# Gate one-hots laid token by token in unit step, in a decoder trunk with product-key experts

## The chip, the cores and the metric

The kernel runs on one core of one Trainium2 chip. The metric is the device time of one execution in microseconds (us); lower is better. The five engines of the core have short names in the profile: PE is TensorE (PEld its weight loads), DVE is VectorE, ACT is ScalarE, POOL is GpSimd and SP is SyncE, which here only issues DMA transfers. Each engine works through its own list of instructions in order and waits on semaphores for the others.

## What is computed

A trunk of two layers over 512 tokens of width 1024. Layer 0 mixes tokens with a gated linear recurrence, layer 1 with latent attention; behind each comes a PEER layer, and this is the part that matters here. For every token and each of 8 heads, two small products with 128 keys each give two top-16 lists, and the best 16 of their sums give 16 experts out of 128 x 128 (index `e1 * 128 + e2`) with softmax gates. Each expert is one neuron, a row of `u_tab` and a row of `v_tab`:

```python
idx = e1 * N_KEYS + e2
g = jax.nn.softmax(cv, axis=-1).astype(h.dtype)
act = jax.nn.gelu(jnp.einsum('bcd,bchkd->bchk', hc, u_tab[ic]), approximate=False)
return jnp.einsum('bchk,bchkd->bcd', gc * act, v_tab[ic])
```

So each token uses 8 x 16 = 128 experts of 16384.

## The kernel before, in words

The kernel treats the four blocks of 128 tokens in two ways. For the last block it gathers the rows of the 128 chosen experts by indirect DMA (`gather_steps`, L1443), one expert of all 128 tokens per step, and VectorE does the dot product (L1457) or the weighted sum (L1462). For the other three blocks (384 tokens) it computes all 16384 experts densely on TensorE: in 128 steps `u_part` (L1111) multiplies 128 rows of the first table with the tokens and applies the GELU, and 128 steps of the last stage multiply the result by the gates (`weigh`, L1220) and by the second table (`v_part`, L1268). For that it needs the gates as a dense matrix, 128 x 128 per token, nearly all zero.

fp32 operands are split into a high and a low part of reduced fp32 (`split`, L162: L164 on ScalarE, L165 on VectorE), and three matmuls (L201 to L203) do one product. Each `u_part` loads 512 KB of the table (`raw`), splits it into `whi` and `wlo`, and runs 24 matmuls of 384 columns.

**The gate stage.** `gate_prep` (L990) runs once per block. It turns the indices e1, e2 and the gates g of 128 tokens, which lie with tokens on the partitions, by TensorE so that the 128 choices lie on the partitions and the tokens along the free dimension. ScalarE copies e1 and e2 out of PSUM as fp16 (L998, tile `et`) and the gates as fp32 (`gt`, L1001). VectorE writes the gates as two fp16 tiles that add up to them: rounded (L1004) and the rest (L1005), tile `gp`.

`gate_group` (L1008) builds the dense gates of 16 tokens in two halves of HT = 8 tokens. For each half VectorE does two operations of 2048 columns:

- L1022 writes `oo`: for each token and each of the 128 possible values, 1 where the index equals the value and else 0; 8 tokens x 128 values for e1, and the same for e2. The values come from the constant `iota_e`.
- L1024 writes `pr`: the e1 one-hots times the rounded gates, and times their rest.

Then TensorE does, per token, two matmuls of 128 x 128 in fp16 that add up in PSUM: the e2 one-hots as weights, the two halves of `pr` as the moving operand (L1032, and L193 in the helper `follow`). Four tokens fill a bank `wps`, ScalarE copies it into `stg` (L1035), and 16 tokens at a time go to scratch memory in DRAM (L1037). `oo` and `pr` have two buffers each, so a half can be written only when TensorE is done with the half before the last.

In memory the free dimension of `oo` and `pr` is ordered: group of 4 tokens, value, token within the four. The operand of one token (`oo[:, n4 + a, :, t]`, `pr[:, a, :, t]`) thus has a step of 4 elements, 8 bytes. VectorE reads the token operand of L1022 and L1024 as 4 neighbours, repeated over 128 values.

**Order of the work.** Per layer there are 24 calls of `gate_group`. Between them `peer` (L1196 to L1209) puts in two or three `u_part` each (50 over the stage), the decoding of the next block's choices, and 74 of the 256 gather steps of the last block. The order on each engine comes from the order of issue in the program, priorities and a timeline that the tile framework keeps; `issue_after` adds single constraints. `fill` (L253) runs matmuls on `iota_e` whose result is not used, between the layers.

Of the kernel before, what the change touches and what calls it, by code (L numbers as in the profile page):

```python
# [12 lines left out]
F16 = mybir.dt.float16  # L13
I32 = mybir.dt.int32
U32 = mybir.dt.uint32
AF = mybir.ActivationFunctionType
OP = mybir.AluOpType
# [4 lines left out]
P = 128  # L22
# [16 lines left out]
TG = 16  # L39
# [11 lines left out]
HT = 8  # L51
# [32 lines left out]
class Trunk:  # L84
# [25 lines left out]
    def setup(self):  # L110
        nc, c, io = self.nc, self.consts, self.io
        self.csil = c.tile([P, D], F32, name="csil")
        nc.scalar.dma_start(self.csil, bass.AP(tensor=io["c"].tensor, offset=io["c"].offset, ap=[[0, P], [1, D]]))
        self.x = self.state.tile([P, KC, T], F32, name="x")
        for k in range(0, KC, 2):
            nc.sync.dma_start(self.x[:, k:k + 2, :], io["xT"][:, k:k + 2, :])
        self.vecs = c.tile([P, NV], F32, name="vecs")
        nc.scalar.dma_start(self.vecs, io["vecs"])
        self.cst = c.tile([P, 4], F32, name="cst")
        nc.scalar.dma_start(self.cst, io["cst"])  # L120
        ii = c.tile([P, P], I32, name="ii")
        nc.gpsimd.iota(ii, pattern=[[1, P]], base=0, channel_multiplier=-1)
        self.ident = c.tile([P, P], F32, name="ident")
        nc.vector.tensor_scalar(self.ident, ii, 0.0, None, op0=OP.is_equal)
        self.ones = c.tile([P, 1], F32, name="ones")
        nc.vector.memset(self.ones, 1.0)
        self.iota_e = c.tile([P, P, 4], F16, name="iota_e")
        nc.gpsimd.iota(self.iota_e, pattern=[[1, P], [0, 4]], base=0, channel_multiplier=0,
                       allow_small_or_imprecise_dtypes=True)
        self.iota_m = c.tile([P, TOPK, TOPK], BF, name="iota_m")  # L130
        nc.gpsimd.iota(self.iota_m, pattern=[[1, TOPK], [0, TOPK]], base=0, channel_multiplier=0,
                       allow_small_or_imprecise_dtypes=True)
        self.eps = c.tile([P, 1], F32, name="eps")
        nc.vector.memset(self.eps, EPS)
        self.tiny = c.tile([P, 1], F32, name="tiny")
        nc.vector.memset(self.tiny, 1e-30)
        self.mod = c.tile([P, 112], F32, name="mod")
        self.xscr = self.dram.tile([P, KC, T], F32, name="xscr")
        self.gscr = self.dram.tile([DEPTH, SPILL, P, ND], F32, name="gscr")
        self.rscr = self.dram.tile([P, T], F32, name="rscr")  # L140
        self.mscr = self.dram.tile([P, NB, T], BF, name="mscr")
        self.wscr = self.dram.tile([DEPTH, NSG, P, P * TG], F32, name="wscr")
# [108 lines left out]
        return self.last_sq  # L251

    def fill(self, bank, n):  # L253
        e = self.iota_e.rearrange("p e t -> p (e t)")
        for _ in range(n):
            with self.tc.issue_after(self.tail):
                self.tail = self.nc.tensor.matmul(bank, e[:, :P], e, start=True, stop=True).ins
# [732 lines left out]
    def gate_prep(self, pool, e1, e2, g):  # L990
        nc = self.nc
        tp = self.bank("et")
        fl = "p h k -> p (h k)"
        for n, src in enumerate((e1, e2, g)):
            nc.tensor.transpose(tp[:, n * P:n * P + P], src.rearrange(fl), self.ident)
        by_group = [P, P // HT, 2, HT]
        et = pool.tile(by_group, F16, name="et", bufs=2)
        nc.scalar.activation(et.rearrange("p g a t -> p a g t"), tp[:, 0:2 * P].rearrange("p (a g t) -> p a g t", a=2, t=HT),  # L998
                             AF.Copy)
        gt = pool.tile([P, P], F32, name="gt", bufs=2)  # L1000
        nc.scalar.activation(gt, tp[:, 2 * P:3 * P], AF.Copy, scale=GSCALE)  # L1001
        gp = pool.tile(by_group, F16, name="gp", bufs=2)
        gt = gt.rearrange("p (g t) -> p g t", t=HT)
        nc.vector.tensor_copy(gp[:, :, 0, :], gt)  # L1004
        nc.vector.tensor_tensor(gp[:, :, 1, :], gt, gp[:, :, 0, :], op=OP.subtract)  # L1005
        return et, gp

    def gate_group(self, pool, l, b, sg, et, gp):  # L1008
        nc = self.nc
        n4 = HT // 4  # L1010
        shp = [P, 2 * n4, P, 4]
        io = self.iota_e.unsqueeze(1).to_broadcast(shp)
        stg = pool.tile([P, P, TG], F32, name="stg", bufs=2)
        for t0 in range(0, TG, HT):

            def toks(ap):
                g = ap[:, (sg * TG + t0) // HT].rearrange("p q t -> p (q t)")
                return g.rearrange("p (a t) -> p a t", t=4).unsqueeze(2).to_broadcast(shp)

            oo = pool.tile(shp, F16, name="oo", bufs=2)  # L1020
            pr = pool.tile(shp, F16, name="pr", bufs=2)
            nc.vector.tensor_tensor(oo, io, toks(et), op=OP.is_equal)  # L1022
            two = [P, 2, n4, P, 4]
            prod = nc.vector.tensor_tensor(pr.rearrange("p (q a) e t -> p q a e t", q=2),  # L1024
                                           oo[:, 0:n4].unsqueeze(1).to_broadcast(two),
                                           toks(gp).rearrange("p (q a) e t -> p q a e t", q=2), op=OP.mult)
            for a in range(n4):
                wps = self.bank("wps")
                for t in range(4):
                    w = oo[:, n4 + a, :, t]  # L1030
                    out = wps[:, t * P:t * P + P]
                    lead = nc.tensor.matmul(out, w, pr[:, a, :, t], start=True, stop=False).ins  # L1032
                    last = self.follow(lead, out, w, pr[:, n4 + a, :, t], stop=True)
                c = t0 + 4 * a
                nc.scalar.activation(stg[:, :, c:c + 4].rearrange("p e t -> p t e"),  # L1035
                                     wps.rearrange("p (t e) -> p t e", t=4), AF.Copy, scale=1.0 / GSCALE)
        nc.scalar.dma_start(self.wscr[l, b * (P // TG) + sg], stg.rearrange("p e t -> p (e t)"))  # L1037
        return last.ins, prod.ins
# [519 lines left out]
```

## Time and profile before

| | |
|---|---|
| Time, median of 3 runs | 3019.38 us (3011.92 to 3022.08) |
| The profiled execution | 3019.97 us, span 3018.1 us, mean granted clock 0.993 |
| Busy of the span | PE 98%, DVE 85%, ACT 46%, POOL 29% |
| Gate matmuls (L1032 and L193) | 2 x 768, from 468.0 to 2305.0 us |
| One-hots and products (L1022 and L1024) | 96 each, mean 1221 and 1219 ns |
| Copies out of PSUM (L1035) | 192, mean 1113 ns |
| DMA over the span | 813.71 MB, mean 270 GB/s |

A row of a group names line, engine, operation, output <- inputs, the shape as partitions x elements, the count; behind the bar stand busy time in us and the mean of one in ns, then the idle time of the engine just before them and what ended most of it. A row of one line or tile gives the shortest, median and longest duration in ns, then the first and the last start in us. A row of waits reads "engine, what waited, its line <- who released it: us in total, times, longest us". A row of windows gives start and end, then the length, the busy time of each engine with its count of instructions, the granted clock, the share of DMA and GB/s. A row of the chain in time order gives start, length and the line; a row of the timeline gives start, length from the first start to the last end, line, and how many instructions it merges.

### The profile page before, as it was taken

To read this page: it belongs to the slowest core of one execution; us is meant where nothing else is said; L and a number is where in the kernel's file an instruction comes from. 1 tells how busy PE (TensorE), PEld (TensorE's weight loads), DVE (VectorE), ACT (ScalarE), POOL (GpSimd) and SP (SyncE) were. 2 spreads that over 40 slices of the span, in tenths; PEclk is the share of its full clock that TensorE was granted. 3 is DMA by queue.
4 is the path that set the end of the run, shared out by engine and by line. 5 is a ranking of instruction groups with operands and counts; after the bars stand their busy time and mean duration, and the time that the engine had idled before them with its cause. 6 is when DMAs were issued, how large, how long until landed. Compare 5 with 4: busy or idle time off the path is not lost.

```text
span 3018.1 us, 43873 instructions
## 1 busy us (share of the span) xinstructions
PE 2958.0 (98%) x15680; PEld 2648.6 (88%) x15680; DVE 2565.2 (85%) x4887; ACT 1389.1 (46%) x2033; POOL 888.1 (29%) x718
## 2 busy tenths in 40 slices
PE   7999999999999999999999999999999999999998
PEld 5689999999888889998878799999999888899997
DVE  8989999898888878879878888989986777788888
ACT  4752255555433333333576742456554333333333
POOL 4000003344132234535334400023432111145542
PEclk9999999999999999999999999999999999999999
DMA  8544558899999999999324333379999999999996
GB/s 315 181 144 147 185 194 306 299 349 324 311 383 359 361 321 349 326 348 323 120 83 128 121 124 129 126 242 333 319 329 322 320 332 331 320 320 355 345 338 222
DMA packets 296218, 813.71 MB, mean 270 GB/s; under 512 B 33152, under 2 KB 130560, under 8 KB 289600
## 3 DMA queue, kind: packets, MB, share of 16 engines
q1 hardware_dynamic: 188928, 439.41, 42.8%
q0 software_dynamic: 78912, 287.34, 27.0%
q10 hardware_dynamic: 28160, 84.14, 7.1%
q8 instruction: 124, 2.03, 0.3%
q14 instruction: 94, 0.77, 0.1%
HBM read 727.44 MB, written 83.36 MB: 269 GB/s over the span
## 4 chain that ended last, share of the span: by engine, by line
PE 81%; DVE 11%; DMA 3%; issue 2%; ACT 2%; POOL 0%; ACTq 0%; SPq 0%; DVEq 0%; POOLq 0%
PE acc L203 12%; PE acc L202 12%; PE acc L201 11%; PE u L201 10%; PE u L202 10%; PE u L203 10%; PE wps L1032 3%; PE wps L193 3%; DVE wlo L165 2%; DVE ada_junk L153 1%; PE pq L202 1%; PE pq L203 1%; PE pq L201 1%; DMA ada_raw<-in_adaw_dram 1%; PE pv L834 1%
## 5 line engine op out<-in xcount | busy, mean ns | idle before, releaser
L1453 POOL DMA_INDIRECT grow<-in_u_dram,idx x256 | 361.2, 1411 | 1140.5 <-DVE gdot L1457 419.7
L201 PE MATMUL u<-h,wlo 128*128 128x384 f32 x2048 | 691.8, 338 | 1.7 <-ACT gact L1128 1.0
L203 PE MATMUL u<-h,whi 128*128 128x384 f32 x2048 | 688.1, 336 | 0.0
L202 PE MATMUL u<-h,whi 128*128 128x384 f32 x2048 | 687.2, 336 | 0.0
L203 PE MATMUL acc<-vh,ah 128*128 128x512 f32 x1512 | 589.4, 390 | 0.0
L202 PE MATMUL acc<-vl,ah 128*128 128x512 f32 x1512 | 589.1, 390 | 0.0
L201 PE MATMUL acc<-vh,al 128*128 128x512 f32 x1512 | 556.5, 389 | 0.0
L1453 POOL DMA_INDIRECT grow<-in_v_dram,idx x256 | 352.7, 1378 | 601.3 <-DVE gacc L1462 397.9
L165 DVE TENSOR_TENSOR wlo<-raw,whi 128x1024 fp32r<-128x1024 f32 (+1 forms) x313 | 383.1, 1225 | 100.7 <-ACT whi L164 99.5
L165 DVE TENSOR_TENSOR vl<-vraw,vh 128x1024 fp32r<-128x1024 f32 x252 | 308.5, 1224 | 118.1 <-ACT vh L164 117.1
L164 ACT ACTIVATE whi<-raw 128x1024 fp32r<-128x1024 f32 (+2 forms) x362 | 352.4, 975 | 120.4 <-issue 32.4
L201 PEld LDWEIGHTS u<-h,wlo 128*128 128x128 f32 x2048 | 386.5, 189 | 5.8 <-ACT gact L1128 1.7
L202 PEld LDWEIGHTS u<-h,whi 128*128 128x128 f32 x2048 | 386.0, 188 | 2.7
L203 PEld LDWEIGHTS u<-h,whi 128*128 128x128 f32 x2048 | 385.5, 188 | 0.1
L203 PEld LDWEIGHTS acc<-vh,ah 128*128 128x128 f32 x1512 | 283.8, 188 | 59.3
L1462 DVE SCALAR_TENSOR_TENSOR gacc<-grow,gdot,gacc 128x1024 f32<-128x1024 f32 x254 | 325.1, 1280 | 11.6 <-DMA grow<-in_v_dram,idx 10.6
L202 PEld LDWEIGHTS acc<-vl,ah 128*128 128x128 f32 x1512 | 283.8, 188 | 57.4
L201 PEld LDWEIGHTS acc<-vh,al 128*128 128x128 f32 x1512 | 283.8, 188 | 56.8
L1457 DVE CUSTOM_DVE_ANT_0 grow<-grow,hn 128x1024 f32<-128x1024 f32 x256 | 309.5, 1219 | 17.0 <-DMA grow<-in_u_dram,idx 16.8
L164 ACT ACTIVATE vh<-vraw 128x1024 fp32r<-128x1024 f32 x252 | 264.4, 1049 | 97.8 <-issue 80.9
L164 ACT ACTIVATE ah<-gact 128x384 fp32r<-128x384 f32 x204 | 106.6, 522 | 380.5 <-PE acc L203 274.7
L1035 ACT ACTIVATE stg<-wps 128x512 f32<-128x512 f32 x192 | 188.1, 1113 | 42.1 <-PE wps L193 41.7
(417 smaller groups left out, 4537.9 us busy)
## 6 DMA issues: line engine op xcount, KB each, us to landing
raw<-in_uT_dram SPq DMA_DIRECT2D x256, 512.0 KB, 5.3
vraw<-in_v_dram SPq DMA_DIRECT2D x256, 512.0 KB, 6.5
wscr<-stg ACTq DMA_DIRECT2D x48, 1024.0 KB, 7.0
wt<-wscr SPq DMA_DIRECT2D x42, 1024.0 KB, 11.0
ada_raw<-in_adaw_dram SPq DMA_DIRECT2D x76, 512.0 KB, 4.5
gscr<-gsp ACTq DMA_DIRECT2D x132, 192.0 KB, 5.4
gact<-gscr SPq DMA_DIRECT2D x108, 192.0 KB, 6.9
ada_raw<-in_adaw_dram POOLq DMA_DIRECT2D x36, 512.0 KB, 6.2
```

The lines of the kernel that those rows point to most:

```text
L153: nc.vector.tensor_tensor_reduce(junk, raw, self.csil, op0=OP.mult, op1=OP.add, scale=1.0, scalar=b, accum_out=col)
L164: last = nc.scalar.activation(hi, src, AF.Copy)
L165: lo = (eng or nc.vector).tensor_tensor(lo, src, hi.bitcast(F32), op=OP.subtract)
L193: return pe.add_instruction(mybir.InstMatmult(name=self.nc.get_next_instruction_name(), start_tensor_calc=start, stop_tensor_calc=stop, ld ...
L201: nc.tensor.matmul(out, al, bh, start=first, stop=False, **kw)
L202: nc.tensor.matmul(out, ah, bl, start=False, stop=False, **kw)
L203: last = nc.tensor.matmul(out, ah, bh, start=False, stop=last, **kw)
L1032: lead = nc.tensor.matmul(out, w, pr[:, a, :, t], start=True, stop=False).ins
L1035: nc.scalar.activation(stg[:, :, c:c + 4].rearrange("p e t -> p t e"), wps.rearrange("p (t e) -> p t e", t=4), AF.Copy, scale=1.0 / GSCALE)
L1453: nc.gpsimd.indirect_dma_start(out=row, out_offset=None, in_=tabs[s], in_offset=bass.IndirectOffsetOnAxis(ap=idx[:, k:k + 1], axis=0))
L1457: nc.vector.tensor_tensor_reduce(row, row, hn, op0=OP.mult, op1=OP.add, scale=1.0, scalar=0.0, accum_out=col)
L1462: nc.vector.scalar_tensor_tensor(acc, row, col, acc, op0=OP.mult, op1=OP.add)
```

## The change

The two tiles of the gate stage get another order in memory, and so do their inputs.

- `iota_e` holds the values 0 to 127 four times in a row, where each value stood four times in a row. `gate_group` reads one such row.
- `gate_prep` writes each index and each gate twice, side by side (a last dimension of 2). ScalarE does so in two instructions of 256 columns, one for e1 and one for e2, where one wrote both with 256 columns in all. The two VectorE operations on the gates write 256 columns for 128.
- `gate_group` orders `oo` and `pr`: index (or half of the gate), token, value. The 128 values of a token lie in unit step, for the weights and for the moving operand. VectorE goes over pairs of values: the token operand is the doubled entry, repeated 64 times.
- `fill` names the dimensions of `iota_e` anew.

The counts of the VectorE operations, matmuls, copies out of PSUM and DMA transfers of `gate_group` stay, as do its buffers.

```diff
-        self.iota_e = c.tile([P, P, 4], F16, name="iota_e")
-        nc.gpsimd.iota(self.iota_e, pattern=[[1, P], [0, 4]], base=0, channel_multiplier=0,
+        self.iota_e = c.tile([P, 4, P], F16, name="iota_e")
+        nc.gpsimd.iota(self.iota_e, pattern=[[0, 4], [1, P]], base=0, channel_multiplier=0,
...
-        by_group = [P, P // HT, 2, HT]
+        by_group = [P, P // HT, 2, HT, 2]
         et = pool.tile(by_group, F16, name="et", bufs=2)
-        nc.scalar.activation(et.rearrange("p g a t -> p a g t"), tp[:, 0:2 * P].rearrange("p (a g t) -> p a g t", a=2, t=HT),
-                             AF.Copy)
+        for n in range(2):
+            src = tp[:, n * P:n * P + P].rearrange("p (g t) -> p g t", t=HT)
+            nc.scalar.activation(et[:, :, n], src.unsqueeze(3).to_broadcast([P, P // HT, HT, 2]), AF.Copy)
...
-        gt = gt.rearrange("p (g t) -> p g t", t=HT)
-        nc.vector.tensor_copy(gp[:, :, 0, :], gt)
-        nc.vector.tensor_tensor(gp[:, :, 1, :], gt, gp[:, :, 0, :], op=OP.subtract)
+        gt = gt.rearrange("p (g t) -> p g t", t=HT).unsqueeze(3).to_broadcast([P, P // HT, HT, 2])
+        nc.vector.tensor_copy(gp[:, :, 0], gt)
+        nc.vector.tensor_tensor(gp[:, :, 1], gt, gp[:, :, 0], op=OP.subtract)
...
-        n4 = HT // 4
-        shp = [P, 2 * n4, P, 4]
-        io = self.iota_e.unsqueeze(1).to_broadcast(shp)
+        shp = [P, 2, HT, P // 2, 2]
+        io = self.iota_e[:, 0].rearrange("p (e d) -> p e d", d=2).unsqueeze(1).unsqueeze(1).to_broadcast(shp)
+        by_pair = "p q t (e d) -> p q t e d"
...
-            nc.vector.tensor_tensor(oo, io, toks(et), op=OP.is_equal)
-            two = [P, 2, n4, P, 4]
-            prod = nc.vector.tensor_tensor(pr.rearrange("p (q a) e t -> p q a e t", q=2),
-                                           oo[:, 0:n4].unsqueeze(1).to_broadcast(two),
-                                           toks(gp).rearrange("p (q a) e t -> p q a e t", q=2), op=OP.mult)
-            for a in range(n4):
+            oo = pool.tile([P, 2, HT, P], F16, name="oo", bufs=2)
+            pr = pool.tile([P, 2, HT, P], F16, name="pr", bufs=2)
+            nc.vector.tensor_tensor(oo.rearrange(by_pair, d=2), io, toks(et), op=OP.is_equal)
+            hot = oo[:, 0].rearrange("p t (e d) -> p t e d", d=2).unsqueeze(1).to_broadcast(shp)
+            prod = nc.vector.tensor_tensor(pr.rearrange(by_pair, d=2), hot, toks(gp), op=OP.mult)
+            for a in range(0, HT, 4):
...
-                    w = oo[:, n4 + a, :, t]
+                    w = oo[:, 1, a + t]
                     out = wps[:, t * P:t * P + P]
-                    lead = nc.tensor.matmul(out, w, pr[:, a, :, t], start=True, stop=False).ins
-                    last = self.follow(lead, out, w, pr[:, n4 + a, :, t], stop=True)
+                    lead = nc.tensor.matmul(out, w, pr[:, 0, a + t], start=True, stop=False).ins
+                    last = self.follow(lead, out, w, pr[:, 1, a + t], stop=True)
```

More of the change, by code (lines that the diff above doesn't have):

```diff
@@ L253, in fill @@
     def fill(self, bank, n):
-        e = self.iota_e.rearrange("p e t -> p (e t)")
+        e = self.iota_e.rearrange("p n e -> p (n e)")
         for _ in range(n):
@@ L1016, in toks @@
             def toks(ap):
[L1017 to L1022, printed above, removed]
-            two = [P, 2, n4, P, 4]
-            prod = nc.vector.tensor_tensor(pr.rearrange("p (q a) e t -> p q a e t", q=2),
-                                           oo[:, 0:n4].unsqueeze(1).to_broadcast(two),
-                                           toks(gp).rearrange("p (q a) e t -> p q a e t", q=2), op=OP.mult)
-            for a in range(n4):
+                return ap[:, (sg * TG + t0) // HT].unsqueeze(3).to_broadcast(shp)
+            oo = pool.tile([P, 2, HT, P], F16, name="oo", bufs=2)
[4 more added lines that the diff above has]
+            for a in range(0, HT, 4):
                 wps = self.bank("wps")
                 for t in range(4):
-                    w = oo[:, n4 + a, :, t]
+                    w = oo[:, 1, a + t]
                     out = wps[:, t * P:t * P + P]
-                    lead = nc.tensor.matmul(out, w, pr[:, a, :, t], start=True, stop=False).ins
-                    last = self.follow(lead, out, w, pr[:, n4 + a, :, t], stop=True)
-                c = t0 + 4 * a
+                    lead = nc.tensor.matmul(out, w, pr[:, 0, a + t], start=True, stop=False).ins
+                    last = self.follow(lead, out, w, pr[:, 1, a + t], stop=True)
+                c = t0 + a
                 nc.scalar.activation(stg[:, :, c:c + 4].rearrange("p e t -> p t e"),
```

## Prediction

> **What bounds the kernel now.** I read the page first: its head, the busy row and the chain that ended last.
>
> ```profile
> span 3018.1 us, 43873 instructions
> PE 2958.0 (98%) x15680; PEld 2648.6 (88%) x15680; DVE 2565.2 (85%) x4887; ACT 1389.1 (46%) x2033; POOL 888.1 (29%) x718
> PE 81%; DVE 11%; DMA 3%; issue 2%; ACT 2%; POOL 0%; ACTq 0%; SPq 0%; DVEq 0%; POOLq 0%
> ```
>
> TensorE is the bound nearly everywhere, with VectorE not far behind. The change touches only the gate stage of each of the two PEER layers, so what it is worth must be read there. By the groups, the gate matmuls (wps) run from 468 to 2305 us in two stretches; I took 461 to 753 and 2010 to 2305 and asked for the busy times in these windows, then for the waits of VectorE in the first and the second, then for those of TensorE in the same order.
>
> ```profile
> core 0: us, PE busy (x) PEld busy (x) DVE busy (x) ACT busy (x) POOL busy (x), PEclk, DMA share, GB/s
> 461.00:753.00 292.00, 285.44 (x1865) 279.09 (x1864) 260.41 (x309) 166.14 (x203) 118.14 (x69) 0.99 0.91 321
> 2010.00:2305.00 295.00, 290.13 (x1907) 283.21 (x1906) 259.69 (x303) 168.53 (x205) 111.17 (x69) 0.99 0.92 323
> ```
> ```profile
> DVE oo L1022 <- PE wps L193: 18.0, 15, 2.9
> DVE wlo L165 <- ACT whi L164: 11.4, 11, 3.4
> DVE grow L1457 <- DMA grow<-in_u_dram,idx: 1.7, 2, 1.3
> ```
> ```profile
> DVE oo L1022 <- PE wps L193: 20.1, 16, 2.6
> DVE wlo L165 <- ACT whi L164: 8.5, 11, 2.1
> DVE grow L1457 <- DMA grow<-in_u_dram,idx: 5.2, 1, 5.2
> DVE g L949 <- PE et L995: 1.3, 1, 1.3
> ```
> ```profile
> PE wps L1032 <- DVE pr L1024: 6.4, 5, 2.0
> ```
> ```profile
> PE wps L1032 <- DVE pr L1024: 4.8, 3, 3.7
> ```
>
> In these 587 us TensorE is busy for 97 to 98%, VectorE for 88 to 89%. Most of VectorE's idle time is the wait to write a new oo, because both buffers still hold one-hots that TensorE has not used: 18.0 and 20.1 us. TensorE waits little for VectorE (6.4 and 4.8 us). So TensorE sets the pace and VectorE follows some 32 us per stage (292.0 - 260.4) behind it.
>
> **TensorE: unit step in the gate matmuls.** The number of matmuls (2 x 768) and their sizes stay. What one costs now is read from the chain, in a run of 32 of them (first, last, and the matmul behind):
>
> ```profile
> 560.25 0.13 PE wps L1032
> ...
> 563.93 0.12 PE wps L193
> 564.05 0.18 PE u L201
> ```
>
> (564.05 - 560.25) / 32 = 0.119 us each, for 128 columns of fp16 with 4 elements between neighbours, in both operands. The nearest fp16 rows in unit step are the two warm filler matmuls of 512 columns:
>
> ```profile
> L257 PEld LDWEIGHTS <-iota_e x11: 95/151/181, 1463.5 to 1472.0; 128*128 128x128 f16 x11
> L257 PE MATMUL rs<-iota_e x2: 377/378/378, 1467.2 to 1467.4; 128*128 128x512 f16 x2
> ```
> ```profile
> 1467.17 0.59 PE L257 MATMUL rs<-iota_e 128*128 128x512 f16 x2
> ```
> ```profile
> L193 PEld LDWEIGHTS <-oo 128*128 128x128 f16 x768 | 90.7, 118 | 6.9 <-issue 5.6
> L1032 PEld LDWEIGHTS <-oo 128*128 128x128 f16 x768 | 89.5, 117 | 18.2 <-DVE pr L1024 9.6 <-issue 5.7 <-DVE wlo L165 0.5
> ```
>
> The second filler starts 0.59 - 0.378 = 0.212 us after the first, so 512 unit-step columns stream in 0.212 us and 128 would in 0.053. The strided matmul takes over twice that. Its weight load is also longer than the unit-step one, 117 to 118 against 95 ns. Both fit strided reads at about half rate. The new cost of one is bounded by 0.053 us below (only the stream counts) and 0.119 above (a load and a matmul of this size take that in any layout). Between them lies 0.097, if each matmul waits for the record of its load to end, as the strided ones seem to (load 0.118, spacing 0.119). That it need not is seen on fp32 weights, whose load records are longer than the spacing:
>
> ```profile
> L1171 PEld LDWEIGHTS sc<-keys,pq_s x256: 187/192/193, 217.8 to 1919.0; 128*128 128x128 f32 x128
> ```
> ```profile
> 1771.83 2.17 PE L1171 MATMUL sc<-keys,pq_s 128*128 128x128 f32 x18
> ```
>
> (18 in 2.17 us is at most 0.121 us each against a load record of 0.192.) I take the middle of 0.053 and 0.097, 0.075 us: TensorE then needs 768 x (0.119 - 0.075) = 34 us less in each stage.
>
> **What is late next: VectorE.** It has 32 us of idle time in the first stage and 35 in the second, so it becomes the bound. Of that idle time only the wait for a free oo goes; the wait for the weight split on ScalarE (11.4, 8.5) and for gathers (1.7, 5.2) has nothing to do with the gate matmuls. So the gain is what VectorE waited for TensorE: 18.0 + 20.1 = 38.1 us. Any matmul cost up to 0.119 - 20.1 / 768 = 0.093 us gives this, so the doubt about 0.053 or 0.075 hardly matters; at 0.097 TensorE saves 17 us per stage, 34 in all, less what doesn't overlap. If nearly all of VectorE's idle time closed (31.6 + 35.3 less 1.7 + 5.2 for gathers), it would be 60 us; that is the low end.
>
> DMA is third. One window shows what it can carry:
>
> ```profile
> 600.00:650.00 50.00, 49.55 (x334) 48.32 (x333) 48.68 (x64) 28.95 (x35) 23.52 (x16) 1.00 0.98 358
> ```
>
> The first stage moves 292 x 321 = 93.7 MB; at 358 GB/s that is 262 us. The forecast stage is 274 us. It fits, tightly.
>
> **VectorE: the two big operations.** 96 of each; both keep 2048 columns per partition.
>
> ```profile
> L1022 DVE TENSOR_TENSOR oo<-iota_e,et 128x2048 f16<-128x2048 f16 x96 | 116.3, 1221 | 38.3 <-PE wps L193 38.1
> L1024 DVE TENSOR_TENSOR pr<-oo,gp 128x2048 f16<-128x2048 f16 x96 | 115.6, 1219 | 0.0
> L165 DVE TENSOR_TENSOR wlo<-raw,whi 128x1024 fp32r<-128x1024 f32 x311 | 379.1, 1220 | 100.3 <-ACT whi L164 99.1 <-DMA wfirst<-wscr 0.9
> L978 DVE TENSOR_TENSOR oh<-iota_m,rc 128x1024 bf16<-128x1024 bf16 x32 | 22.0, 687 | 0.2
> ```
>
> 2048 columns of fp16 take what 1024 of fp32 take: two per tick. Today the token operand comes in runs of 4 adjacent fp16 values; after, in runs of 2, the same pair 64 times over. Stored twice, every tick still finds two neighbours. Bounds: below, nothing faster is in reach, since a dense 1024 (687 ns) is already at the same two per tick; above, one per tick, 2 x 1220 less the fixed part 2 x 687 - 1220 = 154 ns, which is 2.29 us, or +1.07 each. I take +0, by the nearest rows: fp32 operations whose operand is one 4-byte word read again and again (L929, each of 4 values over 16 columns) against one with nothing repeated (L1005).
>
> ```profile
> L929 DVE TENSOR_TENSOR cand<-v x32: 264/274/287, 228.2 to 1963.3; 128x128 f32<-128x128 f32 x32
> ```
> ```profile
> L1005 DVE TENSOR_TENSOR gp<-gt,gp x6: 279/284/285, 466.1 to 2213.8; 128x128 f16<-128x128 f32 x6
> ```
>
> 274 against 284 ns: re-reading a word costs nothing. A pair of fp16 is one such word.
>
> **The small parts.** Per block of 128 tokens (6 in all) gate_prep now issues two ScalarE copies that write 256 columns each, where one did; and its two VectorE operations write 256 columns for 128.
>
> ```profile
> L998 ACT ACTIVATE et<-et x6: 371/384/423, 460.0 to 2209.8; 128x256 f16<-128x256 f32 x6
> ```
> ```profile
> L1004 DVE CAST gp<-gt x6: 218/219/221, 463.4 to 2210.7; 128x128 f16<-128x128 f32 x6
> ```
> ```profile
> L947 DVE CAST i4f<-iu x8: 266/286/343, 379.4 to 2053.2; 128x256 bf16<-128x256 uint32 x8
> ```
>
> ScalarE: +0.384 x 6 = 2.3 us, under its 43% of idle time but for the first block of each stage, whose oo waits for et: 0.8. VectorE: a 256-column cast takes 286 (+0.07), the subtraction 284 + 128 more columns at one per tick (1.04 ns, from 1220 - 687 over 512) = 417 (+0.13): 6 x 0.2 = 1.2. Sum 2.0 us, all counted. The iota in the new order, and the filler matmuls that read it, have the same sizes: 0. No DMA, no wait and no queue changes; scratch rows go out as before.
>
> **Sum.** The profiled execution took 3019.97 us, 1.9 more than its span: 3019.97 - 38.1 + 2.0 = 2983.9. The median of the runs shown (3019.38) lies 0.6 lower: 2983.3, so I say 2983.
>
> **Rivals.** (1) Layout is nothing to TensorE: 0.119 us is the price of a load and a matmul of 128 columns. For it: load record (118) and spacing (119) agree to a nanosecond. Against: the 95 ns load in unit step, and that a load record need not be waited out. Time: 3019.4 + 2.0 = 3021. A step of 4 fp16 elements still puts two of them in each 16 bytes, and the Trainium skill (Advanced Engine Details and Errata, Memory Cachelines) says two hits on a 16-byte line are enough for full speed; by that rule this rival holds. The 95 against 117 ns speak against it here, though no run here has both operands in unit step at 128 columns. Chance 0.12.
>
> (2) Slower: VectorE pays for pairs. The token operand no longer brings 8 adjacent bytes but one 4-byte word per tick. If that costs half of the way to one per tick, 0.53 us, the 192 operations take 102 us more; VectorE is then the bound, the 38 us come off, and the rest stays: 3019 + 102 - 38 + 2 = 3085. It decides from 38 / 192 = 0.20 us per operation on. For it: no row shows runs of two. Against: L929. The Trainium skill (Vector Engine (DVE) Microarchitecture Reference, section 5.2 on measured stream behaviour) has a port at full rate only for runs of at least two adjacent 4-byte words, and some 0.7 ns more per element for others; by that, 0.7 us per operation and about 3120 us. L929 doesn't show it for a repeated word. Chance 0.11.
>
> **How the numbers follow.** Forecast 0.77 (with its cases at 0.097 us, near 2995, and the low end 3019 - 60 + 2 = 2961), rival 1 0.12, rival 2 0.11. The range from 2961 to 3019 leaves out rival 2 and most of rival 1. A change below 0.3% (9 us) can't be told from none. Faster 0.77, same 0.12, slower 0.11.
>
> **What would show it.** Right: gate matmuls below 0.095 us apart with a load record near 95 ns; oo and pr still at 1.22 us; the wait of oo for TensorE nearly gone and TensorE's wait for pr grown to some 20 us per stage; each stage about 19 us shorter, everything else as it was. Wrong: spacing still 0.119 (rival 1), pr or oo above 1.4 us (rival 2), VectorE's wait for DMA or for whi grown by as much as oo's shrank, or another order of the instructions on an engine.

## The result, and the profile after

| | before | after |
|---|---|---|
| Median of 4 runs each | 3018.06 us | 2970.03 us (2963.21 to 2974.67) |
| The profiled execution, its span | 3019.97, 3018.1 us | 2963.21, 2961.4 us |
| Mean granted clock | 0.993 | 0.990 |

After stands to before as 0.9841, with a 95% interval of 0.9814 to 0.9867: 48 us less by the medians, with an interval of some 40 to 56. The forecast was 36 less. The profiled execution of after was the fastest of its four, 6.8 us below their median, and that of before lay 1.9 above the median here, so the 56.7 us between the two spans overstate the gain by some 9 us.

The page's head, busy row and chain of after:

```profile
span 2961.4 us, 43899 instructions
PE 2874.9 (97%) x15680; PEld 2566.0 (87%) x15680; DVE 2559.4 (86%) x4887; ACT 1387.6 (47%) x2039; POOL 960.9 (32%) x718
PE 72%; DVE 15%; issue 5%; DMA 4%; POOL 2%; ACT 2%; ACTq 0%; DVEq 0%; SPq 0%; POOLq 0%
```

TensorE has 83 us less busy time, VectorE 6 us less, and VectorE's share of the chain went from 11 to 15%. By the starts in the trace, from the first `oo` of a layer to the last gate matmul, the stages took 298.0 and 303.7 us before and take 267.8 and 274.5 after: 30.2 and 29.2 less. Elsewhere the last stage of layer 0 grew by 4.2 us (668.4 to 672.6), that of layer 1 stayed at 674.8, and the stretch between them took 3.0 less. So the gain is in the two gate stages. For a comparison over whole stages, the windows of before, then those of after (columns as in the prediction: start and end, length, busy PE, PEld, DVE, ACT and POOL, clock, DMA share, GB/s):

```profile
461.00:760.00 299.00, 292.30 (x1913) 285.46 (x1912) 267.41 (x317) 172.12 (x210) 119.82 (x70) 0.99 0.91 321
2001.00:2306.00 305.00, 300.13 (x1965) 293.21 (x1964) 268.60 (x317) 176.72 (x216) 111.70 (x70) 0.99 0.91 318
```
```profile
462.00:731.00 269.00, 250.33 (x1913) 243.22 (x1912) 262.84 (x311) 170.05 (x211) 146.80 (x69) 0.98 0.96 352
1973.00:2249.00 276.00, 259.95 (x1962) 253.81 (x1961) 265.08 (x316) 173.51 (x218) 147.88 (x70) 0.97 0.95 347
```

The two engines have changed places. TensorE is idle for 18.7 and 16.1 us, VectorE for 6.2 and 10.9 where it had been idle for 31.6 and 36.4. The waits of VectorE in the first and the second stage of after, and then those of TensorE in the same order:

```profile
DVE wlo L165 <- ACT whi L164: 4.4, 7, 1.4
DVE grow L1455 <- DMA grow<-in_u_dram,idx: 1.2, 2, 0.8
DVE oo L1022 <- PE wps L193: 0.3, 1, 0.3
```
```profile
DVE grow L1455 <- DMA grow<-in_u_dram,idx: 5.0, 3, 4.4
DVE wlo L165 <- ACT whi L164: 3.8, 3, 2.7
DVE oo L1022 <- PE wps L193: 2.1, 2, 1.2
```
```profile
PE wps L1030 <- DVE pr L1024: 18.3, 11, 5.6
```
```profile
PE wps L1030 <- DVE pr L1024: 15.9, 8, 5.1
```

The wait for a free `oo` is gone (18.0 and 20.1 before), and TensorE now waits for `pr`. But the wait for the weight split on ScalarE shrank too, from 11.4 to 4.4 and from 9.6 to 3.8 (8.5 in the prediction's second window, which begins 9 us later), and that was not forecast. One sign that the prediction had set down as wrong showed as well: the order of the instructions is another one on TensorE, VectorE and ScalarE. What that order is worth is read from m4 below. The timeline of TensorE shows 16 gate matmuls in a row of after, first and last:

```profile
598.44 0.23 PE L1030 MATMUL wps<-pr,oo 128*128 128x128 f16 x1
...
599.28 0.22 PE L193 MATMUL wps<-pr,oo 128*128 128x128 f16 x1
```

(599.28 - 598.44) / 15 = 0.056 us from one to the next, against 0.119. The rows of the tiles of the gate stage, of after:

```profile
L1030 PEld LDWEIGHTS <-oo x768: 95/98/152, 467.3 to 2248.3; 128*128 128x128 f16 x192
L1022 DVE TENSOR_TENSOR oo<-iota_e,et x96: 1173/1221/1232, 462.7 to 2242.8; 128x2048 f16<-128x2048 f16 x96
L1024 DVE TENSOR_TENSOR pr<-oo,gp x96: 1214/1220/1229, 468.3 to 2246.2; 128x2048 f16<-128x2048 f16 x96
L1005 DVE CAST gp<-gt x6: 280/286/291, 464.9 to 2174.1; 128x256 f16<-128x256 f32 x6
L1006 DVE TENSOR_TENSOR gp<-gt,gp x6: 414/418/423, 467.6 to 2176.6; 128x256 f16<-128x256 f32 x6
L1000 ACT ACTIVATE et<-et x12: 372/380/386, 461.2 to 2169.6; 128x256 f16<-128x256 f32 x12
```

VectorE's two big operations cost what they did (1221 and 1220 ns), and a weight load's record lasts 98 ns where it lasted 117.

### The profile page after: what moved, and what is told of

It is laid out like the page before. It is cut to its first block, busy times and chain, and to the rows that moved or that the text cites. A ratio compares the mean times of both kernels' runs of the same rounds, so it can differ in the third digit from the quotient of the medians.

```text
span 2961.4 us, 43899 instructions
## 1 busy us (share of the span) xinstructions
PE 2874.9 (97%) x15680; PEld 2566.0 (87%) x15680; DVE 2559.4 (86%) x4887; ACT 1387.6 (47%) x2039; POOL 960.9 (32%) x718
## 4 chain that ended last, share of the span: by engine, by line
PE 72%; DVE 15%; issue 5%; DMA 4%; POOL 2%; ACT 2%; ACTq 0%; DVEq 0%; SPq 0%; POOLq 0%
PE acc L202 11%; PE acc L203 11%; PE acc L201 11%; PE u L201 8%; PE u L202 8%; PE u L203 8%; DVE wlo L165 3%; POOL grow L1451 2%; DVE oo L1022 1%; DMA grow<-in_u_dram,idx 1%; DVE pr L1024 1%; PE pq L202 1%; PE pq L203 1%; DMA ada_raw<-in_adaw_dram 1%; PE pq L201 1%
## 5 line engine op out<-in xcount | busy, mean ns | idle before, releaser
L1451 POOL DMA_INDIRECT grow<-in_u_dram,idx x256 | 374.8, 1464 | 1099.2 <-DVE gdot L1455 404.4
L1451 POOL DMA_INDIRECT grow<-in_v_dram,idx x256 | 411.6, 1608 | 514.5 <-DVE gacc L1460 336.5
L203 PEld LDWEIGHTS acc<-vh,ah 128*128 128x128 f32 x1512 | 283.8, 188 | 59.2
L202 PEld LDWEIGHTS acc<-vl,ah 128*128 128x128 f32 x1512 | 283.8, 188 | 57.4
L201 PEld LDWEIGHTS acc<-vh,al 128*128 128x128 f32 x1512 | 283.8, 188 | 57.0
L1455 DVE CUSTOM_DVE_ANT_0 grow<-grow,hn 128x1024 f32<-128x1024 f32 x256 | 309.7, 1220 | 20.9 <-DMA grow<-in_u_dram,idx 20.6
```

The costliest lines, as they stand in the source:

```text
L201: nc.tensor.matmul(out, al, bh, start=first, stop=False, **kw)
L202: nc.tensor.matmul(out, ah, bl, start=False, stop=False, **kw)
L203: last = nc.tensor.matmul(out, ah, bh, start=False, stop=last, **kw)
L1451: nc.gpsimd.indirect_dma_start(out=row, out_offset=None, in_=tabs[s], in_offset=bass.IndirectOffsetOnAxis(ap=idx[:, k:k + 1], axis=0))
L1455: nc.vector.tensor_tensor_reduce(row, row, hn, op0=OP.mult, op1=OP.add, scale=1.0, scalar=0.0, accum_out=col)
```

## The experiments

The theories, with the letters that the expectations use where they use letters. **S**: the step of the moving operand set the pace of the gate matmuls. **L**: the step of the weights did, through their load. **V**: in the new stage VectorE is the bound. **D**: it is DMA. All edits are made in after, unless it is said otherwise. A kernel in which only the order of the elements in an operand differs keeps the order of instructions of after on every engine. Where the amount of work differs, the framework's timeline made another order; it is said each time, since it decides what such a run can show. w4, m4, b2, b8 and once were executed once each (before took 3018.80 us beside the first four), so they are read by their spacing and their stages rather than by their total time. The stages of after, w4 and b2, whose order and pace agree, lie within 2.8 us of each other; smaller differences between stages say nothing.

### What a strided operand costs TensorE

**w4: the weights alone at a step of 4.**

```diff
-                    w = oo[:, 1, a + t]
+                    w = oo.rearrange("p q t e -> p (q t e)").rearrange("p (g e d) -> p g e d", e=P, d=4)[:, 2 + (a + t) // 4, :, (a + t) % 4]
```

> The changed kernel, but TensorE reads the weights (the e2 one-hots) at a step of 4 elements out of the same tile, the moving operand in unit step; the weights so read are other elements of the tile, so the gates made are not the reference's. Theory S (stream): the moving operand's step set the old pace of 0.118 us; then the spacing stays near 0.056 us, the load record goes to 115 to 118 ns, and the time stays within 10 us of the changed kernel's 2970. Rival L (load): the load of strided weights set it; spacing 0.118, TensorE needs 768 x 0.062 = 48 us more per stage, time near 3018.

Measured: 2970.98 us, stages of 270.4 and 274.8, spacing 0.056. The load's record:

```profile
L1030 PEld LDWEIGHTS <-oo x768: 111/113/152, 469.1 to 2256.1; 128*128 128x128 f16 x192
```

The record is 15 ns longer (115 to 118 were expected), and the spacing stays. A load of 113 ns under a spacing of 56 lies beside other matmuls. L falls.

**m4: the moving operand alone at a step of 4**, in both matmuls.

```diff
+            pv = pr.rearrange("p q t e -> p (q t e)").rearrange("p (g e d) -> p g e d", e=P, d=4)
...
-                    lead = nc.tensor.matmul(out, w, pr[:, 0, a + t], start=True, stop=False).ins
-                    last = self.follow(lead, out, w, pr[:, 1, a + t], stop=True)
+                    lead = nc.tensor.matmul(out, w, pv[:, 0 + (a + t) // 4, :, (a + t) % 4], start=True, stop=False).ins
+                    last = self.follow(lead, out, w, pv[:, 2 + (a + t) // 4, :, (a + t) % 4], stop=True)
```

> The changed kernel, but TensorE reads the moving operand (the products) at a step of 4 elements out of the same tile, the weights in unit step; the products so read are other elements of the tile, so the gates made are not the reference's. Theory S: spacing 0.107 to 0.118 us at a load record of 95 to 98 ns, time near 3015. Rival L: spacing 0.056, time near 2970. If both operands count, it lies between, near 0.085, and the time is near 2975, since VectorE then still sets the pace (up to 0.093 us it should cost nothing).

Measured: 3025.40 us, spacing 0.116. The timeline has 31 gate matmuls from the first to the last of these rows, 30 steps of 0.116 us; below them the load's record, whose weights lie in unit step here, and the waits of VectorE in the first stage:

```profile
601.17 0.30 PE L193 MATMUL wps<-pr,oo 128*128 128x128 f16 x1
...
604.65 0.30 PE L193 MATMUL wps<-pr,oo 128*128 128x128 f16 x1
```
```profile
L1031 PEld LDWEIGHTS <-oo x768: 95/115/133, 467.0 to 2310.3; 128*128 128x128 f16 x192
```
```profile
DVE oo L1022 <- PE wps L193: 18.8, 16, 2.1
DVE wlo L165 <- ACT whi L164: 14.8, 15, 4.9
```

This one edit brings the stages back to 299.5 and 303.7 us (before 298.0 and 303.7) and both waits of VectorE with them. S is shown. Two things follow besides. The load's record has a median of 115 ns though its weights are as in after, where 95 to 98 were expected: it grows with the matmuls beside it as well as with the step of the weights (w4), so by itself it doesn't tell what a load costs. And m4 has all of the new preparation, the new order of the instructions and the new reading of pairs, and its stages are 1.5 and 0.0 us longer than those of before: within the stages these cost next to nothing, and the new order is not what made the gain. The last stage of layer 0 is another matter: it takes 673.3 us in m4 and 668.4 in before.

**b2 and b8: both operands at a step of 2, and of 8.** The same edit with `d=2` and `d=8` in the weights and in the moving operand, for example:

```diff
+            pv = pr.rearrange("p q t e -> p (q t e)").rearrange("p (g e d) -> p g e d", e=P, d=8)
...
-                    lead = nc.tensor.matmul(out, w, pr[:, 0, a + t], start=True, stop=False).ins
+                    lead = nc.tensor.matmul(out, w, pv[:, 0 + (a + t) // 8, :, (a + t) % 8], start=True, stop=False).ins
```

> The changed kernel, but TensorE reads both operands at a step of 2 elements (4 bytes) out of the same tiles; other elements than they should be, so the gates made are not the reference's. If any step other than 1 halves the rate: spacing 0.118, load record 117 ns, time near 3018. If it depends on how many elements lie in 8 bytes (two at a step of 2, one at a step of 4): spacing 0.056, time near 2970.

> The changed kernel, but TensorE reads both operands at a step of 8 elements (16 bytes) out of the same tiles; other elements than they should be, so the gates made are not the reference's. If a step costs the same whatever its length: spacing 0.118, load record 117 ns, time near 3018. If the cost grows with the step, because one element lies in each 16 bytes where two did at a step of 4: spacing about 0.23 us, load record near 150 ns; TensorE then needs 768 x 0.17 = 131 us more per stage than in the changed kernel, time near 3190.

Measured: b2 2964.40 us, stages 270.6 and 272.9; b8 3271.39 us, stages 416.5 and 422.5. Their timelines, 10 matmuls (9 steps) of b2 and 21 (20 steps) of b8:

```profile
597.82 0.22 PE L1031 MATMUL wps<-pr,oo 128*128 128x128 f16 x1
...
598.34 0.22 PE L193 MATMUL wps<-pr,oo 128*128 128x128 f16 x1
```
```profile
597.82 0.42 PE L193 MATMUL wps<-pr,oo 128*128 128x128 f16 x1
...
602.49 0.41 PE L193 MATMUL wps<-pr,oo 128*128 128x128 f16 x1
```

That is 0.058 and 0.234 us. Steps of 1, 2, 4 and 8 fp16 elements thus cost 0.056, 0.058, 0.116 and 0.234: up to a step of 2 (four of the elements read in each 16 bytes) the matmul has all but its full pace, and each doubling of the step beyond that doubles the time. The figure for 4 is m4's, with the moving operand alone; at 8 no run tells the two operands apart. Nor does a run show whether 16 bytes are the unit, since none has another element size or a longer step. b8 came out slower than the 3190 us expected, with 148.7 and 147.9 us more per stage for 131; its clock, at the end of this document, has a part in that.

**m4h: only the matmul with the rounded gates at a step of 4**, so that the pace of the two lies between; it was made against the prediction's sentence that any cost up to 0.093 us gives the same gain.

```diff
+            pv = pr.rearrange("p q t e -> p (q t e)").rearrange("p (g e d) -> p g e d", e=P, d=4)
...
-                    lead = nc.tensor.matmul(out, w, pr[:, 0, a + t], start=True, stop=False).ins
+                    lead = nc.tensor.matmul(out, w, pv[:, 0 + (a + t) // 4, :, (a + t) % 4], start=True, stop=False).ins
```

> The changed kernel, but one of the two matmuls of a token (the one with the rounded gates) reads its moving operand at a step of 4 elements out of the same tile; the gates made are not the reference's. The mean spacing is then (0.056 + 0.116) / 2 = 0.086 us, below the 0.093 from which the prediction had VectorE alone set the pace. If that step of the prediction holds, the time stays within 6 us of the changed kernel's 2970. If TensorE's time still counts in part (it waits for pr, then is late for the next u), the 768 x 0.030 = 23 us per stage come through by a third to a half: 2985 to 2993.

Measured: 2997.26 us (2993.65 to 2999.52), 0.993 of before (0.9907 to 0.9952); stages 283.7 and 286.4. Twelve strided matmuls with the eleven others between them, and the window and VectorE's waits of the first stage:

```profile
598.30 0.28 PE L1031 MATMUL wps<-pr,oo 128*128 128x128 f16 x1
...
600.20 0.28 PE L1031 MATMUL wps<-pr,oo 128*128 128x128 f16 x1
```
```profile
464.00:748.00 284.00, 269.79 (x1908) 263.79 (x1907) 264.12 (x311) 169.58 (x211) 114.07 (x69) 0.98 0.93 334
```
```profile
DVE oo L1022 <- PE wps L193: 9.1, 13, 1.7
DVE wlo L165 <- ACT whi L164: 7.7, 8, 2.5
```

(600.20 - 598.30) / 22 = 0.086 us. That is below 0.093, and still the stages are 15.9 and 11.9 us longer than in after, for 768 x 0.030 = 23 us more of TensorE: two thirds and a half of it come through, where a third to a half was expected. The matmul's cost is not free up to 0.093 us. With one and the same order on every engine, a spacing of 0.116, 0.086 and 0.056 us leaves VectorE waiting 18.8, 9.1 and 0.3 us for `oo` and 14.8, 7.7 and 4.4 us for `whi` in the first stage: both waits follow TensorE.

### What the doubling is for

**once: index and gate stored once**, read by VectorE as one element again and again.

```diff
-        by_group = [P, P // HT, 2, HT, 2]
+        by_group = [P, P // HT, 2, HT]
...
-        shp = [P, 2, HT, P // 2, 2]
+        shp = [P, 2, HT, P]
...
-            nc.vector.tensor_tensor(oo.rearrange(by_pair, d=2), io, toks(et), op=OP.is_equal)
+            nc.vector.tensor_tensor(oo, io, toks(et), op=OP.is_equal)
```

> The changed kernel with each index and gate stored once: unit step for TensorE, but VectorE reads one token value again and again (step 0) over 128 columns. If VectorE then does one column per tick: oo and pr take 2.29 us each, 96 x 1.07 = 103 us more per stage, time near 3170. If the doubling isn't what keeps it at two per tick: 1.22 us and 2970.

Measured: 3193.37 us, stages 393.2 and 379.6, in another order of the instructions.

```profile
L1021 DVE TENSOR_TENSOR oo<-iota_e,et x96: 2273/2279/2331, 463.6 to 2468.3; 128x2048 f16<-128x2048 f16 x96
L1023 DVE TENSOR_TENSOR pr<-oo,gp x96: 2233/2279/2287, 471.8 to 2473.8; 128x2048 f16<-128x2048 f16 x96
```

2279 against 1221 ns, beside the prediction's upper bound of 2.29 us: one element per tick. The second copy of each index and gate is what keeps VectorE at two; without it the new layout loses some 175 us instead of winning 48. The stages grew by 125.4 and 105.1 us over those of after, where 103 each was expected; this order differs from after's, so only the durations of the two operations are compared like with like.

### What bounds the stage now

**hop_a and hop_b: VectorE made slower in after and in before, by the same amount.** Every fourth weight split of the gate stage reads its fp32 input at a step of 8 elements. Nothing else in the program changes, and each keeps the order of the kernel that it is made from.

```diff
+        if hop:
+            src = src.rearrange("p k m -> p (k m)").rearrange("p (m k) -> p k m", k=KC)
...
-                hi, lo = self.wtile(io["uT"][l][t], KC, eng=nc.vector)
+                hi, lo = self.wtile(io["uT"][l][t], KC, eng=nc.vector, hop=after is not None and t % 4 == 0)
```

> The changed kernel with every fourth weight split of the gate stage made slower on VectorE: it reads raw at a step of 8 fp32 elements, so these low parts are taken from other elements and the output isn't the reference's. Sizes, counts, waits and the order on every engine are the changed kernel's. Some 13 splits per stage take x us longer in all (to be read from the trace; no row before shows this step). Theory V (VectorE sets the pace of the changed gate stage): each stage gets longer by 0.7 x to x. If TensorE still sets it: by less than 0.4 x.

> The same slower splits in the kernel before, with its order on every engine. TensorE sets the pace there and VectorE sits idle for some 32 us per stage. Theory V: the stages get longer by less than 0.4 x. If VectorE's work counted in both kernels alike: by the same share of x as in the changed kernel.

Measured: hop_a 2994.22 us (2992.03 to 2995.20), 0.9917 of before (0.99 to 0.9933), stages 277.5 and 287.0. hop_b 3024.08 us, 1.0025 of before (1.0014 to 1.0037), stages 299.9 and 308.7. The windows of hop_a, then of hop_b:

```profile
465.00:743.00 278.00, 252.13 (x1903) 245.03 (x1902) 271.88 (x310) 169.90 (x210) 164.36 (x69) 0.96 0.94 339
1991.00:2279.00 288.00, 262.69 (x1959) 254.91 (x1958) 275.16 (x315) 174.25 (x218) 167.72 (x69) 0.96 0.93 331
```
```profile
461.00:762.00 301.00, 293.96 (x1908) 286.89 (x1907) 276.95 (x315) 171.34 (x210) 134.03 (x70) 0.98 0.90 319
2003.00:2313.00 310.00, 303.29 (x1964) 296.05 (x1963) 278.34 (x313) 174.83 (x212) 133.13 (x71) 0.98 0.89 314
```

VectorE has 9.0 and 10.1 us more of busy time than in after, and 9.5 and 9.7 more than in before. Such a load lengthens the stages by 9.7 and 12.5 us in after, and by 1.9 and 5.0 in before. The x of the expectations, the added time of the 12 and 13 slower splits, is 10.5 and 11.9 us in hop_a and 11.3 and 12.5 in hop_b, so the shares are 0.9 and 1.1 against 0.2 and 0.4; the second lies just above the range that was set for V, the last on its bound. So VectorE's work counts in full now and was mostly hidden then: V is shown. Not all of the second stage's 12.5 us is the slower splits. GpSimd's issue of one gather takes 16.2 us in the first stage of hop_a and 17.7 in the second, where after has 4.9 and 6.2 at most, and VectorE then waits 4.3 and 5.9 us for rows of `v_tab`, which it never does in the stages of after. The waits of VectorE in hop_b's first stage show where the load went, into the idle time that TensorE had left it (18.0 and 11.4 us in before):

```profile
DVE oo L1024 <- PE wps L195: 13.3, 11, 2.9
DVE wlo L167 <- ACT whi L164: 9.0, 8, 3.4
```

**half: less work for VectorE.** Only the product with the rounded gates is made, and TensorE reads it twice.

```diff
-            prod = nc.vector.tensor_tensor(pr.rearrange(by_pair, d=2), hot, toks(gp), op=OP.mult)
+            prod = nc.vector.tensor_tensor(pr[:, 0:1].rearrange(by_pair, d=2), hot[:, 0:1], toks(gp)[:, 0:1], op=OP.mult)
...
-                    last = self.follow(lead, out, w, pr[:, 1, a + t], stop=True)
+                    last = self.follow(lead, out, w, pr[:, 0, a + t], stop=True)
```

> The changed kernel without the product of one-hots and the gates' rest: VectorE multiplies 1024 columns for 2048, and TensorE reads the first product twice, so the count of matmuls, copies and DMA stays but the gates lack their low part. It takes 48 x 0.53 = 26 us per stage from VectorE and nothing from any other engine or from DMA. Theory V (VectorE is the bound of the changed gate stage): the stages get shorter until TensorE, busy 250 and 260 us in them, is the bound again: by 12 to 18 us each, time 2934 to 2946. Rival D (DMA, at a share of 0.96, is the bound): the stages shorten by less than 4 us each, time 2962 to 2970.

Measured: 2998.89 us (2995.77 to 3003.96), 0.9941 of before (0.9923 to 0.996). That is some 29 us slower than after, with less to do. Its first window, and TensorE's largest wait behind the stage:

```profile
462.00:714.00 252.00, 236.74 (x1829) 229.85 (x1829) 222.17 (x291) 161.26 (x200) 105.42 (x59) 0.98 0.93 344
```
```profile
PE ot L1341 <- DVE gacc L1460: 22.2, 1, 22.2
```

The stages are shorter (252.0 and 264.3), but GpSimd has only 59 instructions in the first where it has 69 in after: the order was made anew, and fewer gather steps of the last block lie in the stage. They come later, and at the end of layer 0 TensorE waits 22.2 us for the last gathered expert. That wait is 3.3 us in after:

```profile
PE ot L1341 <- DVE gacc L1460: 3.3, 1, 3.3
```

The gap from the last gate matmul to the last stage grew too, from 29 to 43 us. So with less work on VectorE the stage is shorter, by 15.8 and 10.2 us (12 to 18 were expected), but how much of that is the missing product and how much the missing gathers this run can't say.

**early58a: fewer gather steps in the gate stage**, 58 for 74.

```diff
-EARLY = 74
+EARLY = 58
```

> The changed kernel with 58 gather steps in each gate stage for 74; the other 16 (some 1.25 us of VectorE each) move to the last stage of the layer, where TensorE is the bound. Theory V: each gate stage loses 16 x 1.25 = 20 us of VectorE work and gets 12 to 18 us shorter; the last stages stay within 3 us, time 2934 to 2950. Rival D: 16 gathers are also 8 MB less DMA, some 9% of the stage, so it would help here too; told apart by the run with half the products. If the last stage pays for them, the time stays near 2970.

Measured: 2995.35 us (2992.29 to 2998.39), 0.9926 of before (0.9903 to 0.995); stages 269.5 and 269.9, and again the wait of TensorE for the last gathered expert at the end of layer 0, this time 22.3 us. The order was made anew here as well. Taking gathers out gained nothing in the first stage and 4.6 us in the second, and layer 0 gave back more at its end: its last stage took 691.9 us for 672.6. Neither of the times that were expected came.

**poolw: every sixth weight split of the stage on GpSimd** for VectorE.

```diff
-                hi, lo = self.wtile(io["uT"][l][t], KC, eng=nc.vector)
+                hi, lo = self.wtile(io["uT"][l][t], KC, eng=nc.gpsimd if after is not None and t % 6 == 0 else nc.vector)
```

> The changed kernel with every sixth weight split of the gate stage on GpSimd, which takes 2.4 us for one (trace of before, three of 1024 columns) where VectorE takes 1.2. It takes some 8 x 1.15 = 9 us per stage from VectorE and gives GpSimd, which also issues the gathers, 19 us more. Theory V: the stages get 4 to 9 us shorter, time 2952 to 2962, if the gathers stay on time. If a split on GpSimd makes TensorE or the gathers wait: 2970 or more.

Measured: 2988.32 us (2982.06 to 2989.02), 0.9891 of before (0.9874 to 0.9908); stages 268.7 and 266.2, so +0.8 and -8.3 us against after, in another order, and a wait for the last gathered expert once more, of 16.3 us. A split on GpSimd took 2.4 to 5.5 us here, where 2.4 was expected, and five of the one-hots and products beside such splits took 3.3 to 3.4 us for 1.2.

None of the three beats after, and none keeps its order, so they don't decide between V and D. The trace of after does, as far as its own stages go. In both of them the waits of the four engines that compute name a DMA only for gathered rows, 1.2 and 5.0 us of VectorE; none waits for a block of the table. It is the queue of these blocks that waits, for VectorE to free a buffer (first stage):

```profile
SPq L178 <- DVE wlo L165: 222.4, 42, 12.8
```

So at a share of 0.96 DMA still follows VectorE, and D falls as the bound of the new stage. That a heavier VectorE lengthens the stage is shown. What a lighter one would bring, and whether DMA would then be the bound, stays open, since no run made VectorE lighter with all else in place.

## Why the prediction was right, and where its terms were off

**The matmul: mechanism right, size off.** The prediction took 0.075 us, the middle between the bare stream (0.053) and a waited-out load (0.097). Measured is 0.056: the stream, and hardly anything besides. The upper of the two ends rested on a matmul that waits for its load's record to end; in after the record lasts 98 ns and in w4 113, both under a spacing of 56, so it doesn't. The Trainium skill (TensorE: Matmul & The Clock Gate, section "Wait — 56ns, not 53.3ns?") has 55.6 ns for back-to-back matmuls of 128 columns, which the trace agrees with; its section "Back-to-back issue gap" has some 81 ns for pairs of load and matmul, and these matmuls, each with its own load record, take 56, so that figure doesn't hold here. TensorE's busy time in the stages fell by 42.0 and 40.2 us where 34 was forecast.

**VectorE as the next bound: right, shown by hop_a against hop_b.** TensorE's new wait for `pr`, forecast at some 20 us per stage, is 18.3 and 15.9. Each stage was to get some 19 us shorter; it was 30.2 and 29.2.

**The step that failed is the sentence that only the wait for a free oo goes,** and that the wait for the weight split "has nothing to do with the gate matmuls". It had. The waits of ScalarE in the first stage, of before and of after, were there to be asked for:

```profile
ACT gsp L1123 <- PE u L203: 94.9, 39, 3.5
```
```profile
ACT gsp L1121 <- PE u L203: 65.8, 35, 2.8
```

ScalarE has its GELU (`gsp`) and the splits in one list, and the GELU waits for the matmuls of `u_part`. A split that stands behind it comes late because TensorE is late. Here is one case from the first stage of before; the bracket holds the idle time ahead and what ended it:

```profile
541.13 0.49 ACT L1123 ACTIVATE gsp<-u 128x384 f32<-128x384 f32 x1 [2.90 <-PE u L203]
541.52 1.05 ACT L164 ACTIVATE whi<-raw 128x1024 fp32r<-128x1024 f32 x1
542.61 1.23 DVE L165 TENSOR_TENSOR wlo<-raw,whi 128x1024 fp32r<-128x1024 f32 x1 [0.54 <-ACT whi L164]
```

ScalarE waits 2.90 us for the matmuls of `u_part`, then does the GELU and the split, and VectorE waits 0.54 us for the split. In 17 of the 23 such waits of VectorE in before's two stages, 13.8 of 21.0 us, the split stood right behind a GELU that had waited for `u`. VectorE's wait for `whi` was thus mostly a wait for TensorE at one remove, and m4, m4h and after show it shrinking with the spacing. Of VectorE's 31.6 and 36.4 us of idle time 25.4 and 25.5 went, not 18.0 and 20.1. VectorE's busy time in the windows also fell, by 4.6 and 3.5 us; with the idle time that makes 30.0 and 29.0 us, by which the windows are shorter. Some of this goes with the pace. From the first `oo` to the last `pr` of a stage m4 and after have the same instructions of VectorE in the same order, and their durations add up to 283.6 and 284.7 us in m4 and 283.8 and 285.7 in after; but the time that they cover is 261.7 and 262.3 us in m4 and 259.9 and 260.4 in after. Records of operations that need not wait overlap more. The rest goes with the windows of after, which hold fewer instructions of VectorE (311 for 317 and 316 for 317).

**"Any matmul cost up to 0.093 us gives this": wrong.** m4h at 0.086 gives back 15.9 and 11.9 us per stage. Two engines that use each other's buffers here don't have one bound with a sharp edge: in that first stage VectorE waits 9.1 us for TensorE to free an `oo` and TensorE 14.2 us for `pr`, at different places, and TensorE's time counts in part.

**The small parts: right.** `oo` and `pr` at 1221 and 1220 ns (forecast 1.22 us), the cast 286 (286), the subtraction 418 (417), the copies of ScalarE 380 (384). The 2.0 us that they were to cost agree with m4's 1.5 and 0.0, which is no more than two profiles differ by.

**DMA: it fitted,** as forecast, at 352 GB/s and a share of 0.96, with little left.

**"Everything else as it was": all but 4 us.** The order of the instructions is not as it was, and the last stage of layer 0 took 4.2 us more, with a wait of TensorE of 3.3 us for the last gathered expert that before doesn't have. This goes with the new order and not with the earlier start of that stage: m4, in which it begins 3.8 us later than in before, and b8, in which it begins 124.6 us later, have after's order and wait 3.5 us each.

**The rivals.** Rival 1 (layout is nothing to TensorE) fell with the spacing of 0.056, and m4 runs two fp16 elements per 16 bytes at half the rate, b2 four at all but full rate. The rule of the Trainium skill that stood beside this rival (Advanced Engine Details and Errata, Memory Cachelines: at least two hits on a 16-byte line are needed, which the prediction took as enough) doesn't cover TensorE's moving operand here: two are not enough. Rival 2 (VectorE pays for pairs) fell with 1220 ns: a repeated pair of fp16 is as good as eight adjacent bytes. A single repeated element does cost, all of the way to one per tick: `once`, 2279 ns.

**The sum.** Forecast were 38.1 - 2.0 = 36.1 us. The stages gave 59.4; the first began 1.5 us later, the last stage of layer 0 took 4.2 more and the stretch behind it 3.0 less, which makes the 56.7 between the spans. The stages thus gave what the prediction had put at the low end of its range, where nearly all of VectorE's idle time closes (60 us), though here a fall of VectorE's busy time has a part in it. Before's profiled execution lay 1.9 above the median of the four runs and after's 6.8 below its own, so 48 us are left between the medians.

## What to carry to other kernels

Lay a moving operand of TensorE in fp16 in unit step, or at a step of 2 at most, and let VectorE write whatever order that asks for; if an operand that VectorE repeats then comes out as single fp16 elements (2279 ns for 1220 here), store it twice so that it reads pairs. Before a wait for a third engine is called independent, look at what that engine waits for itself: here ScalarE stood for TensorE. And when two engines hand buffers to each other, don't count a gain as free up to the point at which the other becomes the bound: price the points between by a run.

## What the runs showed of the hardware that was not expected

- A step of 4 fp16 elements in the weights cost TensorE nothing here: record 113 ns, spacing 0.056 us (w4).
- An fp32 input of VectorE at a step of 8 elements makes a split of 1024 columns take some 2.1 us for 1.22 (hop_a).
- VectorE and GpSimd seem to slow each other down. Five of VectorE's one-hots and products went from 1.2 to 3.4 us beside splits on GpSimd (poolw), and GpSimd's busy time in the stages rose from 119.8 and 111.7 us in before (70 instructions each) to 146.8 and 147.9 in after (69 and 70), where VectorE hardly pauses; in m4, which has after's order and before's pace, the first is 109.9 (69). No run was made for this, and the cause is not shown.
- TensorE's clock can be halved while TensorE is never idle. In b8 the windows around one run of gate matmuls (595.2 to 602.5 us) read:

```profile
594.00:598.00 4.00, 4.00 (x20) 2.88 (x20) 2.76 (x3) 1.61 (x3) 0.52 (x2) 1.00 0.80 223
598.00:602.00 4.00, 4.00 (x18) 2.47 (x17) 1.68 (x3) 3.18 (x4) 0.61 (x1) 0.64 0.71 229
602.00:604.00 2.00, 2.00 (x9) 1.80 (x8) 1.06 (x1) 1.21 (x2) 0.00 (x0) 0.50 0.04 16
```

TensorE is busy for all of the time, and the granted clock (behind the engines) falls to 0.50 some 4 us into the slow matmuls; the mean over the kernel is 0.941. The matmuls stay 0.234 us apart through it, so that price is not one of the clock. Part of b8's loss is then the slower clock for the matmuls of `u_part` behind them, which run 0.320 us apart at first and 0.173 ahead of the gate matmuls.
